# One PSUM bank for w and y of a linear recurrence, and a sum over gated branches by an accumulating DMA

## Chip, cores, metric

One core of a Trainium2 chip runs the kernel; the other cores are idle. The metric is the time of one execution on the device, in microseconds (us).

## What is computed

Two blocks of two layers each, in float32, on 256 tokens of width 1024. Each layer of the first block mixes three branches (sparse attention, a short convolution, and the linear recurrence of RWKV-7), then runs a gated feed-forward net. The change touches only this mixing. Cut to it:

```python
def step(state, inp):                       # the recurrence, per token and head (64 x 64 state)
    r_t, w_t, k_t, v_t, ka_t, kb_t = inp
    sa = jnp.einsum('bhvk,bhk->bhv', state, ka_t)
    state = (state * w_t[:, :, None, :] + sa[..., None] * kb_t[:, :, None, :]
             + v_t[..., None] * k_t[:, :, None, :])
    y_t = jnp.einsum('bhvk,bhk->bhv', state, r_t)
    return state, y_t
...
branches = jnp.stack([y_a, y_b, y_c], axis=2)
up = jnp.einsum('bsgc,gcd->bsgd', branches, w_branch[l])
gates = jax.nn.sigmoid(gate_pre + b_gate[l]).reshape(bsz, seq, N_BRANCH, D_MODEL)
mixed = jnp.sum(gates * up, axis=2)
h = h + mixed @ w_out[l]
```

## The kernel before

Weights stream from HBM in loads of up to 1 MB (`weights`, line 172, issued by SyncE). ScalarE (ACT) rounds each half to float32r (`whi`, line 184) and VectorE (DVE) takes the remainder (`wlo`, line 185); a product is then three float32r matmuls (lines 206 to 208 with the features on the partitions, 244 to 246 with the tokens on them). An operand is split in the same way (`split`, lines 198 and 199).

The first block's mixing (`mix`) runs three generators side by side: `rwkv`, `attend` and `bulk`. `bulk` makes the short convolution, then for 4 column pairs j the gate of branch 1 and its product, the gates of branch 2, then gate and product of branch 0, and last, after the recurrence is done, the product of branch 2. `branch` keeps the running sum: the first branch (g = 1) is written to m[j] (line 1035); each later one makes `u` = (tanh + 1) * up on DVE (line 1038) and GpSimd (POOL) adds it to m[j] (line 1039). After branch 2 each m[j] is halved on DVE (line 1083) and split into the operand `mg[j]` of the output projection (`residual`, whose matmuls are lines 244 to 246). The order of the instructions on one engine is set when the program is built, with due times and by dependences, and is not always that of the code; at run time each engine works in order.

The recurrence is done in 4 chunks of 64 tokens (`rw_chain`), 8 heads of 64. `ar` holds per chunk 64 columns for w and 64 for y (128 rows: two heads); `gm` holds masked scores with 128 rows (64 of the unknowns u, then 64 of the values v) and 128 columns (64 for w, 64 for y). In a chunk:

1. w = `ar`(first 64 columns) x old state + `gm`[64:128](first 64 columns) x v, lines 946 and 949, into one PSUM bank; chunk 0 has no state term. DVE copies it (`wsb`, line 951).
2. u = inverse x w, line 955; DVE copies it into rows 0 to 63 of `u2` (line 956); rows 64 to 127 hold v.
3. The new state, line 960, then DVE (lines 965, 966, 968).
4. y = `ar`(last 64 columns) x old state + `gm`(128 rows, last 64 columns) x `u2`, lines 973 and 976, into another bank; ACT copies it to `yc` (line 979).

After every second chunk `rw_finish` runs the group norm on `yc` (DVE with one ACT step; its reciprocal root is `rsqrt`, lines 261 to 271), and at the end `yc` is transposed (line 393) and split: that is the input of branch 2's product. The banks come from pool `rk`, which has two slots; a float32 matmul appears in the trace as two PE instructions.

Of the kernel before, what the change touches and what calls it, by code (L numbers as in the profile page):

```python
# [13 lines left out]
ALU = mybir.AluOpType  # L14
# [486 lines left out]
class Block1:  # L501
# [434 lines left out]
    def rw_chain(self):  # L936

        k, nc = self.k, self.k.nc
        ar, gm, bkt, uv, ti = self.ar, self.gm, self.bkt, self.uv, self.ti
        for c in range(4):  # L940
            s_old, s_new = self.sd[c % 2], self.sd[(c + 1) % 2]
            u2 = uv[c // 2][:, c % 2]
            ps = k.bank(k.rk, 8, 64)
            for hh in range(4):
                if c:
                    nc.tensor.matmul(ps[0:64, 2 * hh:2 * hh + 2], lhsT=ar[hh // 2][:, hh % 2, c, 0:64], rhs=s_old[:, hh], start=True, stop=False)
                for p in range(2):
                    h = 2 * hh + p
                    nc.tensor.matmul(ps[0:64, h], lhsT=gm[c][64:128, 4 * p + hh, 0:64], rhs=u2[64:128, 64 * h:64 * h + 64], start=c == 0, stop=c == 0 or p == 1)  # L949
            wsb = k.temp(8, 64, name="wsb")  # L950
            nc.vector.tensor_copy(wsb[0:64], ps[0:64])
            ps = k.bank(k.rk, 8, 64)
            for h in range(8):
                b = 8 * c + 4 * (h % 2) + h // 2
                nc.tensor.matmul(ps[0:64, h], lhsT=ti[:, b], rhs=wsb[0:64, h], start=True, stop=True)
            nc.vector.tensor_copy(u2[0:64], ps[0:64].rearrange("p a b -> p (a b)"))
            if c < 3:
                ps = k.bank(k.rk, 4, 128)
                for hh in range(4):
                    nc.tensor.matmul(ps[:, hh], lhsT=bkt[c // 2][:, c % 2, 128 * hh:128 * hh + 128], rhs=u2[:, 128 * hh:128 * hh + 128], start=True, stop=True)  # L960
                for p in range(2):
                    q = slice(64 * p, 64 * p + 64)
                    pc = self.pc[q, :, c:c + 1].to_broadcast([64, 4, 64])
                    if c:
                        nc.vector.tensor_tensor(out=s_new[q, :, q], in0=ps[q, :, q], in1=s_old[q, :, q], op=ALU.add)
                        nc.vector.tensor_tensor(out=s_new[q, :, q], in0=s_new[q, :, q], in1=pc, op=ALU.mult)
                    else:
                        nc.vector.tensor_tensor(out=s_new[q, :, q], in0=ps[q, :, q], in1=pc, op=ALU.mult)
            y = k.bank(k.rk, 8, 64)
            o = slice(64 * (c % 2), 64 * (c % 2) + 64)  # L970
            for hh in range(4):
                if c:
                    nc.tensor.matmul(y[o, 2 * hh:2 * hh + 2], lhsT=ar[hh // 2][:, hh % 2, c, 64:128], rhs=s_old[:, hh], start=True, stop=False)
                for p in range(2):
                    h = 2 * hh + p
                    nc.tensor.matmul(y[o, h], lhsT=gm[c][:, 4 * p + hh, 64:128], rhs=u2[:, 64 * h:64 * h + 64], start=c == 0, stop=c == 0 or p == 1)
            if c == 0:
                self.yc = k.slot(2, 512, name="yc")
            nc.scalar.copy(self.yc[o, c // 2].rearrange("p (h d) -> p h d", d=64), y[o])
            yield 8.0  # L980
            if c % 2:
                self.rw_finish(c // 2)
                yield 8.0
        yc = k.operand(2)
        for j in range(2):
            k.split(k.flip_pair([self.yc[:, 0], self.yc[:, 1]], j), *yc[j])
        self.yo = yc
        yield 3.0
# [41 lines left out]
    def branch(self, l, g, j, th, y, m):  # L1030

        k, nc = self.k, self.k.nc
        ps = k.feature_pair(self.w["w_branch"][l, g], 256 * j, y, 4)
        if m is None:
            nc.vector.scalar_tensor_tensor(out=th, in0=th, scalar=1.0, in1=ps, op0=ALU.add, op1=ALU.mult)
        else:
            u = k.temp(2, S, name="up")
            nc.vector.scalar_tensor_tensor(out=u, in0=th, scalar=1.0, in1=ps, op0=ALU.add, op1=ALU.mult)  # L1038
            nc.gpsimd.tensor_tensor(out=m, in0=m, in1=u, op=ALU.add)  # L1039
        return th  # L1040

    def rwkv(self, l):
# [439 lines left out]
```

## Time and profile before

| | us |
|---|---|
| median of 3 runs (1744.5 to 1745.21) | 1744.61 |
| profiled execution | 1742.93 |
| its span, first to last instruction | 1740.9 |
| busy PE / DVE / ACT / POOL | 1700.2 / 1250.7 / 957.2 / 72.4 |

Times in the profile count from the start of the span. A line of the timeline has start, duration, engine, source line, operation, output and inputs, shape, and in brackets how long the engine had been idle before it and what ended that. Consecutive instructions of one kind are merged into one line with their count (x16); the duration is then that of the whole run, and since matmuls are pipelined, their durations overlap. In the shape of a matmul, 64*128 means 64 contraction rows and 128 columns of the loaded operand.

### The profile page before, as it was taken

How to read it: one execution, taken by the hardware profiler on the slowest of the kernel's cores; microseconds unless marked ns; L12 is line 12 of the kernel's file. 1: busy time of each engine (PE TensorE's matmuls, PEld its weight loads, DVE VectorE, ACT ScalarE, POOL GpSimd, SP SyncE). 2: the span in 40 equal slices, each digit the busy share in tenths (PEclk: the TensorE clock that was granted, in tenths of full speed). 3: DMA queues.
4: the chain of work that ended last, by engine and by line, in shares of the span. 5: the costliest groups of instructions: out<-in, count | busy, mean ns of one | idle time of the engine just before them, and what ended most of it. 6: DMA issues, size and time to landing. Idle time of an engine off the chain costs nothing.

```text
span 1740.9 us, 30007 instructions
## 1 busy us (share of the span) xinstructions
PE 1700.2 (98%) x12016; PEld 1539.7 (88%) x12016; DVE 1250.7 (72%) x2464; ACT 957.2 (55%) x1688; POOL 72.4 (4%) x81
## 2 busy tenths in 40 slices
PE   8999899999999999899999999999999999999998
PEld 8988789899989988799899987788899887888997
DVE  6699947789957689757789857576666675666666
ACT  6554633556646544633555556666564566665643
POOL 2000201101000000201000000000000000000000
PEclk9999989999999999899999999999999999999999
DMA  7534323565556444314555565344445554444454
GB/s 229 171 111 128 115 74 101 178 192 186 181 179 209 127 137 129 98 62 146 169 189 177 186 211 170 129 157 142 157 147 172 191 172 144 146 149 158 155 171 134
DMA packets 217371, 268.89 MB, mean 154 GB/s; under 512 B 6570, under 2 KB 170716, under 8 KB 217232
## 3 DMA queue, kind: packets, MB, share of 16 engines
q1 hardware_dynamic: 213520, 262.81, 46.7%
q10 hardware_dynamic: 2944, 3.94, 0.8%
q8 instruction: 94, 1.54, 0.4%
q14 instruction: 45, 0.37, 0.1%
q0 software_dynamic: 768, 0.23, 0.1%
HBM read 265.91 MB, written 1.05 MB: 153 GB/s over the span
## 4 chain that ended last, share of the span: by engine, by line
PE 81%; DVE 11%; DMA 4%; ACT 3%; issue 2%; POOL 0%; ACTq 0%; SPq 0%; POOLq 0%; DVEq 0%
PE ps L206 15%; PE ps L207 15%; PE ps L208 15%; PE ps L246 8%; PE ps L244 8%; PE ps L245 8%; DVE wlo L185 4%; PE ps L445 2%; PE ps L393 2%; DMA raw<-in_ffn_down_dram 1%; DMA raw<-in_w_in_dram 1%; ACT whi L184 1%; PE ps L486 1%; DVE pr L905 1%; PE ps L949 1%
## 5 line engine op out<-in xcount | busy, mean ns | idle before, releaser
L185 DVE TENSOR_TENSOR wlo<-raw,whi 128x1024 fp32r<-128x1024 f32 (+2 forms) x504 | 615.4, 1224 | 302.2 <-ACT whi L184 289.1
L184 ACT ACTIVATE whi<-raw 128x1024 fp32r<-128x1024 f32 (+2 forms) x504 | 525.6, 1046 | 555.9 <-PE ps L207 292.8
L206 PE MATMUL ps<-op,whi 128*128 128x256 f32 x2464 | 710.6, 288 | 0.1
L207 PE MATMUL ps<-op,whi 128*128 128x256 f32 x2464 | 703.3, 285 | 1.2 <-DVE op L199 1.0
L208 PE MATMUL ps<-op,wlo 128*128 128x256 f32 x2464 | 702.2, 285 | 1.3 <-DVE wlo L185 1.2
L206 PEld LDWEIGHTS ps<-op,whi 128*128 128x128 f32 x2464 | 474.8, 193 | 11.2 <-issue 8.5
L207 PEld LDWEIGHTS ps<-op,whi 128*128 128x128 f32 x2464 | 475.2, 193 | 6.6 <-issue 4.3
L208 PEld LDWEIGHTS ps<-op,wlo 128*128 128x128 f32 x2464 | 474.9, 193 | 3.8 <-DVE wlo L185 1.8
L244 PE MATMUL ps<-whi,op 128*128 128x512 f32 (+2 forms) x784 | 306.2, 391 | 0.8 <-ACT qtok L1200 0.8
L245 PE MATMUL ps<-wlo,op 128*128 128x512 f32 (+2 forms) x784 | 302.2, 386 | 2.5 <-DVE wlo L185 2.5
L246 PE MATMUL ps<-whi,op 128*128 128x512 f32 (+2 forms) x784 | 303.2, 387 | 1.3 <-DVE op L199 1.3
L246 PEld LDWEIGHTS ps<-whi,op 128*128 128x128 f32 x784 | 148.5, 189 | 30.0 <-DVE op L199 2.2
L245 PEld LDWEIGHTS ps<-wlo,op 128*128 128x128 f32 x784 | 148.8, 190 | 29.4 <-DVE wlo L185 3.8
L244 PEld LDWEIGHTS ps<-whi,op 128*128 128x128 f32 x784 | 148.6, 190 | 29.4 <-issue 2.0
L454 ACT ACTIVATE e<-e,m 128x128 f32<-128x128 f32 (+1 forms) x160 | 70.9, 446 | 16.2 <-DVE m L451 15.8
L451 DVE CUSTOM_DVE_ANT_0 e<-ps,consts 128x128 f32<-128x128 f32 (+1 forms) x128 | 39.1, 351 | 15.5 <-PE ps L445 13.2
L199 DVE TENSOR_TENSOR op<-xt,op 128x512 fp32r<-128x512 f32 x48 | 32.2, 687 | 19.0 <-ACT op L198 18.8
L445 PE MATMUL ps<-qT 64*128 64x256 f32 (+1 forms) x256 | 35.8, 351 | 1.0 <-DVE m L451 0.8
L488 ACT COPY pt<-ps 128x384 f32<-128x384 f32 x64 | 28.8, 480 | 12.9 <-PE ps L486 7.6
L709 DVE SCALAR_TENSOR_TENSOR glu<-ps,vec,glu 128x254 f32<-128x254 f32 x72 | 34.4, 478 | 1.4
L1039 POOL TENSOR_TENSOR gate<-gate,up 128x512 f32<-128x512 f32 x16 | 26.0, 1627 | 212.3 <-DVE up L1038 169.6
L708 DVE SCALAR_TENSOR_TENSOR glu<-ps,vec,glu 128x255 f32<-128x255 f32 x72 | 34.3, 476 | 0.2
(337 smaller groups left out, 1562.7 us busy)
## 6 DMA issues: line engine op xcount, KB each, us to landing
raw<-in_w_in_dram SPq DMA_DIRECT2D x130, 1024.0 KB, 5.2
raw<-in_ffn_up_dram SPq DMA_DIRECT2D x44, 1024.0 KB, 5.1
raw<-in_ffn_down_dram SPq DMA_DIRECT2D x20, 1024.0 KB, 5.1
raw<-in_w_out_dram SPq DMA_DIRECT2D x16, 1024.0 KB, 5.2
raw<-in_w_branch_dram SPq DMA_DIRECT2D x24, 512.0 KB, 3.4
raw<-in_w_proj_a_dram SPq DMA_DIRECT2D x8, 1024.0 KB, 5.2
raw<-in_w_proj_b_dram SPq DMA_DIRECT2D x8, 1024.0 KB, 5.2
raw<-in_w_in_dram SPq DMA_DIRECT2D x8, 768.0 KB, 4.4
```

Of the source, the lines that this page charges most:

```text
L184: nc.scalar.activation(out=hi, in_=v, func=AF.Copy)
L185: nc.vector.tensor_tensor(out=lo, in0=v, in1=hi.bitcast(F32), op=ALU.subtract)
L206: self.nc.tensor.matmul(ps, lhsT=hi[:, k], rhs=xh, start=k == 0, stop=False)
L207: self.nc.tensor.matmul(ps, lhsT=hi[:, k], rhs=xl, start=False, stop=False)
L208: self.nc.tensor.matmul(ps, lhsT=lo[:, k], rhs=xh, start=False, stop=k == nk - 1)
L244: self.nc.tensor.matmul(ps[t][:, :n], lhsT=xh, rhs=hi, start=kk == first, stop=False)
L245: self.nc.tensor.matmul(ps[t][:, :n], lhsT=xh, rhs=lo, start=False, stop=False)
L246: self.nc.tensor.matmul(ps[t][:, :n], lhsT=xl, rhs=hi, start=False, stop=kk == last)
L393: self.nc.tensor.transpose(ps[:, a, 128 * t:128 * t + 128], src[t][:, 128 * k:128 * k + 128], self.ident)
L445: nc.tensor.matmul(ps[b][:, a:a + n], lhsT=qt[r, 128 * t:128 * t + 128], rhs=kt[r, 0:n], start=True, stop=True)
L451: nc.vector.tensor_tensor_reduce(out=e[:, a:a + n], in0=ps[b][:, a:a + n], in1=mask[:, a:a + n], scale=1.0, scalar=3e38, op0=ALU.add, op1= ...
L454: nc.scalar.activation(out=e[:, a:a + n], in_=e[:, a:a + n], func=AF.Exp, scale=-1.0, bias=m[:, t:t + 1], accum_out=z[:, 2 * b + t:2 * b + ...
```

## The change

In `rw_chain` w and y share one bank `wy`: w's matmuls load all 128 columns of `gm` and `ar`, so that rows 0 to 63 of the bank get w and rows 64 to 127 the part of y that needs only v and the old state. All `gm` matmuls stand together ahead of all `ar` matmuls. When u is known, y gets only the remaining term, with 64 contraction rows. The separate bank and the 4 `ar` matmuls of y in chunks 1 to 3 are gone. In `branch` the POOL add becomes a DMA, issued by POOL, that reads `u` and adds it to m[j] in SBUF.

```diff
-            ps = k.bank(k.rk, 8, 64)
-            for hh in range(4):
-                if c:
-                    nc.tensor.matmul(ps[0:64, 2 * hh:2 * hh + 2], lhsT=ar[hh // 2][:, hh % 2, c, 0:64], rhs=s_old[:, hh], start=True, stop=False)
-                for p in range(2):
-                    h = 2 * hh + p
-                    nc.tensor.matmul(ps[0:64, h], lhsT=gm[c][64:128, 4 * p + hh, 0:64], rhs=u2[64:128, 64 * h:64 * h + 64], start=c == 0, stop=c == 0 or p == 1)
+
+            wy = k.bank(k.rk, 8, 64)
+            for h in range(8):
+                nc.tensor.matmul(wy[:, h], lhsT=gm[c][64:128, 4 * (h % 2) + h // 2], rhs=u2[64:128, 64 * h:64 * h + 64],
+                                 start=h == 0, stop=False, skip_group_check=True)
+            if c:
+                for hh in range(4):
+                    nc.tensor.matmul(wy[:, 2 * hh:2 * hh + 2], lhsT=ar[hh // 2][:, hh % 2, c], rhs=s_old[:, hh],
+                                     start=False, stop=False, skip_group_check=True)
             wsb = k.temp(8, 64, name="wsb")
-            nc.vector.tensor_copy(wsb[0:64], ps[0:64])
+            nc.vector.tensor_copy(wsb[0:64], wy[0:64])
...
-            y = k.bank(k.rk, 8, 64)
             o = slice(64 * (c % 2), 64 * (c % 2) + 64)
-            for hh in range(4):
-                if c:
-                    nc.tensor.matmul(y[o, 2 * hh:2 * hh + 2], lhsT=ar[hh // 2][:, hh % 2, c, 64:128], rhs=s_old[:, hh], start=True, stop=False)
-                for p in range(2):
-                    h = 2 * hh + p
-                    nc.tensor.matmul(y[o, h], lhsT=gm[c][:, 4 * p + hh, 64:128], rhs=u2[:, 64 * h:64 * h + 64], start=c == 0, stop=c == 0 or p == 1)
+            for h in range(8):
+                nc.tensor.matmul(wy[64:128, h], lhsT=gm[c][0:64, 4 * (h % 2) + h // 2, 64:128], rhs=u2[0:64, 64 * h:64 * h + 64],
+                                 start=False, stop=h == 7, skip_group_check=True)
             if c == 0:
                 self.yc = k.slot(2, 512, name="yc")
-            nc.scalar.copy(self.yc[o, c // 2].rearrange("p (h d) -> p h d", d=64), y[o])
+            nc.scalar.copy(self.yc[o, c // 2].rearrange("p (h d) -> p h d", d=64), wy[64:128])
...
             u = k.temp(2, S, name="up")
             nc.vector.scalar_tensor_tensor(out=u, in0=th, scalar=1.0, in1=ps, op0=ALU.add, op1=ALU.mult)
-            nc.gpsimd.tensor_tensor(out=m, in0=m, in1=u, op=ALU.add)
+            nc.gpsimd.dma_start(out=m, in_=u, accum_op=ALU.add)
```

## Rows read from the trace of the kernel before

**Rows 1.** The page: shares of the chain that ended last; the costliest group

```profile
PE 81%; DVE 11%; DMA 4%; ACT 3%; issue 2%; POOL 0%; ACTq 0%; SPq 0%; POOLq 0%; DVEq 0%
...
L185 DVE TENSOR_TENSOR wlo<-raw,whi 128x1024 fp32r<-128x1024 f32 (+2 forms) x504 | 615.4, 1224 | 302.2 <-ACT whi L184 289.1
```

**Rows 2.** Waits of PE: us in total, times, longest

```profile
PE ps L393 <- DVE yc L1020: 2.9, 2, 1.4
...
PE ps L246 <- DVE op L199: 1.3, 2, 0.7
```

**Rows 3.** Timeline of PE, recurrence, chunk 2 of the first layer

```profile
253.82 0.43 PE L946 MATMUL ps<-sd,ar 128*64 128x128 f32 x2
...
254.56 0.43 PE L946 MATMUL ps<-sd,ar 128*64 128x128 f32 x2
...
258.02 1.14 PE L955 MATMUL ps<-wsb,ti 64*64 64x64 f32 x16
260.15 1.06 PE L960 MATMUL ps<-uv,bkt 128*128 128x128 f32 x8
...
261.64 0.38 PE L973 MATMUL ps<-sd,ar 128*64 128x128 f32 x2
...
262.09 0.38 PE L973 MATMUL ps<-sd,ar 128*64 128x128 f32 x2
```

**Rows 4.** Timeline of PE: other small float32 matmuls, and chunk 0

```profile
217.78 0.80 PE L926 MATMUL ps<-t,gm 32*32 32x32 f32 x11
...
610.53 1.18 PE L808 MATMUL ps<-consts,kn 128*128 128x8 f32 x10
...
655.59 1.16 PE L861 MATMUL ps<-ar,bk 64*128 64x128 f32 x16
...
737.76 1.97 PE L949 MATMUL ps<-uv,gm 64*64 64x64 f32 x16
...
745.21 1.91 PE L960 MATMUL ps<-uv,bkt 128*128 128x128 f32 x8
747.06 1.63 PE L976 MATMUL ps<-uv,gm 128*64 128x64 f32 x16
```

**Rows 5.** Windows (us; busy PE, PEld, DVE, ACT, POOL; PEclk; DMA share; GB/s)

```profile
218.00:220.00 2.00, 2.00 (x27) 1.68 (x25) 0.00 (x0) 1.37 (x4) 0.00 (x0) 0.77 0.83 262
...
232.00:234.00 2.00, 2.00 (x24) 1.76 (x23) 0.67 (x2) 0.59 (x2) 0.00 (x0) 0.81 0.00 0
```

**Rows 6.** Timeline of DVE and POOL in the group norm, first layer

```profile
288.83 0.17 DVE L275 TENSOR_SCALAR gn<-gn 128x8 f32<-128x8 f32 x1
...
288.99 1.28 POOL L1039 TENSOR_TENSOR gate<-gate,up 128x512 f32<-128x512 f32 x1 [7.24 <-DVE gn L275]
289.03 1.28 DVE L261 TENSOR_SCALAR rsy<-gn 128x8 int32<-128x8 int32 x1
```

**Rows 7.** Timeline of DVE at the end of the first mixing stage

```profile
300.28 2.17 DVE L185 TENSOR_TENSOR wlo<-raw,whi 128x1024 fp32r<-128x1024 f32 x1 [0.28 <-ACT whi L184]
302.37 0.67 DVE L1038 SCALAR_TENSOR_TENSOR up<-gate,ps 128x512 f32<-128x512 f32 x1
303.16 2.33 DVE L185 TENSOR_TENSOR wlo<-raw,whi 128x1024 fp32r<-128x1024 f32 x1
305.41 0.41 DVE L1083 TENSOR_SCALAR gate<-gate 128x512 f32<-128x512 f32 x1
...
315.60 1.77 DVE L199 TENSOR_TENSOR op<-gate,op 128x512 fp32r<-128x512 f32 x1
```

**Rows 8.** Windows of the same stage

```profile
298.00:311.00 13.00, 13.00 (x109) 12.96 (x108) 10.87 (x13) 5.67 (x8) 4.38 (x3) 1.00 0.58 204
311.00:323.00 12.00, 11.27 (x50) 8.79 (x48) 10.22 (x13) 5.04 (x6) 4.28 (x2) 1.00 0.49 165
```

**Rows 9.** DMA issues: queue, count, KB each, median us to landing

```profile
gup<-in_rw_g_up_dram ACTq DMA_DIRECT2D x2, 256.0 KB, 4.4
...
out_dram<-hg SPq DMA_DIRECT2D x2, 256.0 KB, 2.1
```

## Prediction

> **What bounds the kernel now.** I read the page first. The matrix engine (PE) carries 81% of the chain that ended last, VectorE (DVE) 11% [rows 1]. So an instruction taken from PE gives back its pitch (start to start), not its listed duration, since durations overlap; and a step on another engine counts only where PE stands waiting for it. The change has two places, each once per layer of the first block, so I read those next: the recurrence by the timeline of PE, and the end of the mixing stage by the waits, the timelines of DVE, POOL and PE, and the windows. Around the recurrence other work fills PE's waits, so there the price is PE pitch alone. At the end of mixing PE waits twice in each of the two layers: up to 1.4 us for `yc`, the end of the recurrence, and up to 0.7 us for an operand made from the sum over branches [rows 2].
>
> **w and y in one bank.** Every float32 matmul is two PE instructions. In chunks 1 to 3 the old w is four groups of two `L946` and four `L949`, and a group comes every 0.74 us (253.82 to 254.56), 2.94 us in all. The old y is four groups of two `L973` and four `L976`, 0.45 us each (261.64 to 262.09), 1.80 us in all [rows 3]. The groups of w are longer because PE goes from 128 contraction rows to 64 and back in each of them: 0.74 less 0.45 is some 0.28 us for the two switches.
>
> New w: 16 instructions with 64 rows and 128 columns, then 8 with 128 by 128. No row has the first shape with 64 moving columns. Its pitch is bounded below by 0.06 us, which `L861` shows with two alternating row halves ((1.16 - 0.27) / 15), and above by 0.11 us from `L960` ((1.06 - 0.28) / 7); the nearest is `L808`, 128 columns loaded for 8 moving ones, (1.18 - 0.28) / 9 = 0.10 us [rows 3, 4]. I take 0.10. That is 1.60 + 0.28 + 8 x 0.11 = 2.76 us against 2.94 (bounds 2.1 and 2.9). New y: 16 instructions of 64 by 64 at the pitch of `L955`, (1.14 - 0.22) / 15 = 0.061, plus a switch pair: 0.98 + 0.28 = 1.26 us against 1.80. One chunk gains 0.18 + 0.54 = 0.72 us, and six chunks 4.3 us (bounds 3.5 and 8.3).
>
> Chunk 0 goes the other way. It has no `L946`, so nothing is merged, and its w loads 128 columns where it loaded 64. It also runs on the low clock: the granted clock falls to 1.2 GHz in the stretch from 218 us and is back at 2.4 GHz in that from 232 us [rows 5]; before the fall PE ran matmuls of 32 by 32 [rows 4]. Old w there is 16 at 0.118 = 1.9 us; new w lies between the same 1.9 and 16 x 0.23 = 3.7 us, the pitch of `L960` at that clock ((1.91 - 0.3) / 7) [rows 4]. I take 3.2, nearer the row with as many columns: +1.3 us. Old y there took some 1.4 us (1.63 less one overlap) [rows 4]; new y is 16 x 0.118 = 1.9 us, less if the clock rises within it: +0.5 us (bounds -0.2 and +0.7). Chunk 0 loses 1.8 us (-0.2 to +2.5), two layers 3.6 us. The first part comes to 3.6 - 4.3 = **-0.7 us**, bounds -8.7 and +1.5.
>
> One PSUM slot of the two of `rk` is now held from w to the copy of y. The state update takes the other, which its own input (`u2`) has freed already, so I price that at nothing; were it to wait, the wait would be a VectorE copy, some 0.7 us a chunk.
>
> **The sum by DMA.** Sixteen POOL adds (`L1039`) go and sixteen accumulating DMAs of 256 KB, issued by POOL, come. POOL's other work of the layer (`rw_rows`, the memsets) stands ahead of them and the next layer's far behind, so none of it is delayed. Two effects, per layer:
>
> *What goes.* While POOL adds, DVE work is slow. An eight-column operation of `rsqrt` (`L261`) took 1.28 us beside an add that began 0.04 us earlier; its neighbour took 0.17 us [rows 6]. It lies on the group norm's path to `yc`, for which PE then waits 1.4 us [rows 2]. So 1.1 us of that wait goes: **-2.2 us** for two layers (0 to -2.5; 0 if issuing the DMA blocks DVE as the add does, or if the order of DVE's work changes there).
>
> *What comes.* The four sums of branch 2 are each followed by the halving (`L1083`), the split (ACT, then DVE) and the output projection. Now 2.37 us pass from the end of the product (302.37 + 0.67) to the halving at 305.41 [rows 7]. With a DMA they must hold its issue, its reading of both operands and its landing. No row shows an accumulating DMA. From below: storing 256 KB lands in 2.1 us. From above: a 256 KB load beside other traffic lands in 4.4 us [rows 9], and the second operand is another 256 KB; at full share the traffic here is some 204 / 0.58 = 350 GB/s [rows 8], so 0.75 us alone and 1.5 us shared with the weight loads, hence 6 us. I take 4.5, near the loaded row, since the stage also streams `w_out`.
>
> The halving waits in DVE's queue, and behind it stand the next product, the low halves (`wlo`) of the `w_out` weights and the next split, for which PE waits. From 298 to 323 us DVE is busy for 10.87 + 10.22 = 21.1 of 25 us, so it has 3.9 us idle [rows 8]; without the POOL adds it gets some 3.1 us more: `wlo` at 303.16 takes 2.33 us and at 300.28 2.17, where the mean of its line is 1.22, and the split at 315.60 takes 1.77 us, some 1.1 more than its kind does alone [rows 1, 7]. Four halvings, each 4.5 - 2.37 = 2.1 us later, need 8.5 us; 7.0 are there. So 1.5 us per layer reach PE: **+3.0 us**. At 2.1 us nothing waits, and PE's 0.7 us for the operand goes too: -1.5 us. At 6 us it is 4 x 3.63 - 7.0 = 7.5 us per layer, +15 us. The eight sums of branch 0 have many us until they are read; they cost nothing, and if they did, it would show as a wait of the first halving.
>
> The Trainium skill, DMA: Bandwidth & Descriptors, section "Anatomy of one DMA — SWDGE (gpsimd) path", fits a DMA issued by GpSimd as 2.0 us plus bytes over 436 GB/s. That would be an estimate of 2.6 us here, and by it the last term would be -1.5 instead of +3.0. The trace's loaded rows are slower, and I go by them.
>
> **The sum.** -0.7 - 2.2 + 3.0 = +0.1 us. The profiled execution took 1742.93 us (span 1740.9 and 2.0 around it); the median of the three timed runs lies 1.7 us above it, and I put the sum on the median: **1744.7 us, no change**. This kernel's measurement can tell some 0.2%, 3.5 us, from no change.
>
> **Rivals.** *The DMA is slow (slower).* Place: the four halvings at the end of mixing. It decides from a latency of some 5 us; at 5.3 us the four waits exceed the cover by 4 x 2.93 - 7.0 = 4.7 us a layer, 9.4 us in all, less the 2.9 gained elsewhere 6.5 us: 1751. At 6 us it is 1757. For it: four 1 MB loads of `w_out` are under way in the same 20 us. Against it: the halving already stands behind other DVE work, and the order could put more there. The skill's page SBUF — State Buffer, section "Who interferes with whom", says that descriptors of GpSimd's DMAs are held up by DVE's two-port modes; no row here shows it. Chance 0.26.
>
> *The clock comes back late (slower).* The low stretch ends just after PE ran full-array matmuls (`L960`) and y [rows 4, 5]. The new y has half the rows. If y and the next w stayed at 1.2 GHz, they would cost some 3.5 us per layer more: 1752. Against it: chunk 0's w now fills twice the columns, which could as well bring the clock back sooner. Chance 0.08.
>
> *The DMA is quick (faster).* Near the store's 2.1 us nothing waits: -0.7 - 2.2 - 1.5 = -4.4, 1740; with the low bound of w's pitch as well, 1732. For it: no HBM is read. Chance 0.22. This is also what the skill's fit above would give.
>
> *The change doesn't do what it says:* if other work splits up the merged matmuls in PE's order, the switches stay; the first part then gives up to +3 us, still within the forecast. Chance 0.04, and 0.40 for the forecast itself.
>
> **How the numbers follow.** Faster by over 0.2%: 0.22. Within 0.2%: 0.40 + 0.04 = 0.44. Slower: 0.26 + 0.08 = 0.34. The range takes in most of both sides, 1738 to 1755; it leaves out the double gain below and the slowest DMAs above. The likeliest case's own range is 1741 to 1748.
>
> **What would show it.** In the changed profile: `L949` with 128 columns at a pitch of 0.10 us and y at 0.06; `L261` back at 0.17 us and PE's wait for `yc` near 0.3 us; DVE's wait before `L1083` naming a DMA; that DMA's landing time, 4.5 us, in the list of DMA issues. The prediction is wrong if that landing is under 3 or over 5.3 us, if the granted clock returns at another point of chunk 0 or 1, or if DVE's order changes so that the halving no longer holds anything up.

## The result: slower by 0.7%, and the profile after

The changed kernel takes 1755.76 us (median of four runs, 1752.95 to 1760.66) against 1744.55 us (1742.09 to 1745.21): 11.2 us more, a ratio of 1.0069 with a 95% interval of 1.0052 to 1.0085. The forecast of 1744.7 us was wrong, and its range ended at 1755, 0.8 us short. The profiled execution took 1756.67 us, with a span of 1754.9.

Where the time went is seen first by stage. For each layer of the first block I take two points of PE's timeline: the first `L926`, just ahead of the recurrence, and the first transpose of the new `h` (`L393`), which ends the mixing.

| us | start to `L926` | recurrence to end of mixing, layer 1 | to `L926` of layer 2 | the same stage, layer 2 | rest |
|---|---|---|---|---|---|
| before | 214.8 | 108.3 | 405.8 | 109.4 | 902.6 |
| after | 213.7 | 116.5 | 404.0 | 119.7 | 901.1 |

All of the loss lies in the two stages that the change touches, 8.2 and 10.3 us; elsewhere the profiled execution was a little quicker.

First the page: the shares of the chain, and the row of the new DMA among the issues (count, KB, median us to landing). It lands in 4.2 us, close to the 4.5 that the prediction took, and this median misleads, as will be seen.

```profile
PE 82%; DVE 9%; issue 4%; DMA 3%; ACT 2%; POOL 0%; SPq 0%; POOLq 0%; ACTq 0%; DVEq 0%
...
gate<-up POOLq DMA_DIRECT2D x16, 256.0 KB, 4.2
```

The waits (us in total, times, longest) answer to [rows 2]:

```profile
ACT op L198 <- DVE gate L1081: 22.1, 8, 7.2
DVE gate L1081 <- DMA gate<-up: 17.8, 8, 4.5
PE ps L244 <- ACT op L198: 5.4, 3, 3.0
PE ps L245 <- DVE wlo L185: 4.6, 7, 1.2
PE ps L946 <- ACT yc L977: 1.4, 2, 0.7
PE ps L246 <- DVE op L199: 1.0, 3, 0.3
PE ps L393 <- DVE yc L1018: 0.8, 2, 0.4
```

Two lines of the kernel before, to be held against the second and the fourth:

```profile
DVE gate L1083 <- POOL gate L1039: 4.7, 4, 1.2
PE ps L245 <- DVE wlo L185: 2.5, 4, 1.2
```

Read from the last line up: the wait for `yc` fell from 1.4 to 0.4 us a layer. A new wait of 0.7 us a layer stands before w of chunk 1 (`L946`), and the halving (`L1081`) waits in every one of its eight places for the DMA, behind it ACT for the operand, behind that PE. Behind the operand (`L198`) stand the high halves of the weights (`whi`) in ACT's queue, so in the first layer PE's first long wait names them. The first load of `w_out`, issued at 302.84 us, had landed by then, after 7.0 us.

```profile
311.62 0.63 ACT L198 ACTIVATE op<-gate 128x512 fp32r<-128x512 f32 x1 [7.19 <-DVE gate L1081]
312.16 1.99 ACT L184 ACTIVATE whi<-raw 128x1024 fp32r<-128x1024 f32 x2
313.25 0.50 PE L244 MATMUL ps<-whi,op 128*128 128x512 f32 x1 [1.16 <-ACT whi L184]
```

The timeline of DVE at the end of the first mixing stage, to be held against [rows 7]:

```profile
303.49 0.69 DVE L1036 SCALAR_TENSOR_TENSOR up<-gate,ps 128x512 f32<-128x512 f32 x1 [0.68 <-PE ps L208]
304.46 1.23 DVE L185 TENSOR_TENSOR wlo<-raw,whi 128x1024 fp32r<-128x1024 f32 x1 [0.29 <-ACT whi L184]
306.37 0.69 DVE L1036 SCALAR_TENSOR_TENSOR up<-gate,ps 128x512 f32<-128x512 f32 x1 [0.68 <-PE ps L208]
311.16 0.43 DVE L1081 TENSOR_SCALAR gate<-gate 128x512 f32<-128x512 f32 x1 [4.10 <-DMA gate<-up]
...
314.95 0.43 DVE L1081 TENSOR_SCALAR gate<-gate 128x512 f32<-128x512 f32 x1 [0.49 <-DMA gate<-up]
...
320.59 0.43 DVE L1081 TENSOR_SCALAR gate<-gate 128x512 f32<-128x512 f32 x1 [1.15 <-DMA gate<-up]
...
325.08 0.43 DVE L1081 TENSOR_SCALAR gate<-gate 128x512 f32<-128x512 f32 x1 [2.33 <-DMA gate<-up]
```

Two things are new. The second product (306.37) now stands ahead of the first halving; before, the halving came right behind the low halves. And `wlo` takes 1.23 us where it took 2.17 and 2.33. Next POOL, which issues the sums; the row of SP's loads of `w_out` in the same time; and the windows of two stretches (us; busy PE, PEld, DVE, ACT, POOL; PEclk; DMA share; GB/s):

```profile
301.60 0.85 POOL L1037 DMA_DIRECT2D gate<-up  x1 [9.15 <-DVE up L1036]
304.47 0.85 POOL L1037 DMA_DIRECT2D gate<-up  x1 [2.02 <-DVE up L1036]
307.36 0.85 POOL L1037 DMA_DIRECT2D gate<-up  x1 [2.03 <-DVE up L1036]
316.26 0.85 POOL L1037 DMA_DIRECT2D gate<-up  x1 [8.05 <-DVE up L1036]
318.60 0.86 POOL L1037 DMA_DIRECT2D gate<-up  x1 [1.48 <-DVE up L1036]
...
302.84 19.70 SPq L172 DMA_DIRECT2D raw<-in_w_out_dram  x4
...
306.00:311.00 5.00, 5.00 (x44) 5.00 (x44) 0.69 (x1) 0.00 (x0) 0.85 (x1) 1.00 1.07 288
320.00:325.00 5.00, 3.35 (x11) 2.01 (x10) 2.16 (x3) 1.69 (x2) 0.00 (x0) 0.85 1.05 316
```

The trace gives a landing time for each issue. Earlier in the layer (issues at 269.1, 283.0 and 291.6) they are 4.2, 3.7 and 3.6 us. The five above land after 4.4, 6.7, 7.6, 4.3 and 6.5 us, and the last of the second layer after 8.5: a sum issued 2.3 to 2.9 us behind another takes longer (5.4 to 8.5 us) than one with none ahead (3.6 to 4.4), and the DMA engines are full where the halving waits longest, with DVE busy for 0.69 of 5 us. The loads of `w_out` suffer too: the four of this stage land after 7.0, 10.0, 6.7 and 7.4 us, where the same four took 5.1 to 5.2 in the kernel before. The median of 4.2 is that of a mixed population: half of it are sums of branch 0, most of them in quiet stretches.

Last, the recurrence: PE in chunk 0 and the start of chunk 1 (to 240 us), then chunk 2 of the first layer, and the windows.

```profile
222.14 3.67 PE L946 MATMUL ps<-uv,gm 64*128 64x64 f32 x16
...
232.61 1.97 PE L973 MATMUL ps<-uv,gm 64*64 64x64 f32 x16
235.29 3.67 PE L946 MATMUL ps<-uv,gm 64*128 64x64 f32 x16 [0.72 <-ACT yc L977]
238.89 2.07 PE L950 MATMUL ps<-sd,ar 128*128 128x128 f32 x8
...
258.26 2.00 PE L946 MATMUL ps<-uv,gm 64*128 64x64 f32 x16
260.19 1.16 PE L950 MATMUL ps<-sd,ar 128*128 128x128 f32 x8
...
266.19 1.14 PE L973 MATMUL ps<-uv,gm 64*64 64x64 f32 x16
...
218.00:234.00 16.00, 16.00 (x134) 14.94 (x133) 3.44 (x5) 4.00 (x8) 0.00 (x0) 0.50 0.05 17
234.00:242.00 8.00, 7.28 (x37) 6.88 (x35) 1.37 (x2) 3.37 (x8) 0.00 (x0) 0.53 0.00 0
```

Before, the clock of the first layer was back at 2.4 GHz in the window from 232 us [rows 5]; now it comes back near 241, so w of chunk 1 also runs at 1.2 GHz: 235.29 to 240.62 (the next instruction), 5.3 us, where chunk 2 takes 2.84 (258.26 to 261.10). The second layer goes another way: y of chunk 0 runs at full clock, PE waits 0.72 us, and the clock falls again within w of chunk 1, which takes 4.2 us (755.66 to 759.82).

```profile
753.80 1.14 PE L973 MATMUL ps<-uv,gm 64*64 64x64 f32 x16
755.66 2.50 PE L946 MATMUL ps<-uv,gm 64*128 64x64 f32 x16 [0.72 <-ACT yc L977]
758.09 2.07 PE L950 MATMUL ps<-sd,ar 128*128 128x128 f32 x8
```

Summed over windows of 2 us, PE ran at the low clock for the equivalent of 23.9 us in the first layer and 23.8 in the second (13.7 and 17.1 before).

### The profile page after: what moved, and what is told of

It reads as the page before. It is cut to its first block, busy times and chain, and to the rows that moved or that the text cites. A ratio compares the mean times of both kernels' runs of the same rounds, so it can differ in the third digit from the quotient of the medians.

```text
span 1754.9 us, 29929 instructions
## 1 busy us (share of the span) xinstructions
PE 1706.5 (97%) x11968; PEld 1546.4 (88%) x11968; DVE 1239.6 (71%) x2464; ACT 958.3 (55%) x1688; POOL 61.1 (3%) x81
## 4 chain that ended last, share of the span: by engine, by line
PE 82%; DVE 9%; issue 4%; DMA 3%; ACT 2%; POOL 0%; SPq 0%; POOLq 0%; ACTq 0%; DVEq 0%
PE ps L206 15%; PE ps L207 15%; PE ps L208 14%; PE ps L246 9%; PE ps L244 9%; PE ps L245 9%; DVE wlo L185 2%; PE ps L445 2%; PE ps L393 2%; DMA raw<-in_w_in_dram 1%; PE ps L946 1%; PE ps L486 1%; DVE pr L905 1%; PE ps L496 1%; DMA gate<-up 1%
## 5 line engine op out<-in xcount | busy, mean ns | idle before, releaser
L185 DVE TENSOR_TENSOR wlo<-raw,whi 128x1024 fp32r<-128x1024 f32 (+2 forms) x504 | 608.5, 1210 | 306.5 <-ACT whi L184 289.2
L246 PEld LDWEIGHTS ps<-whi,op 128*128 128x128 f32 x784 | 148.3, 189 | 30.8 <-DVE op L199 2.6
L486 PE MATMUL ps<-ident,e 128*128 128x128 f32 x192 | 31.7, 287 | 3.5 <-DVE m L451 3.5
```

The costliest lines, as they stand in the source:

```text
L185: nc.vector.tensor_tensor(out=lo, in0=v, in1=hi.bitcast(F32), op=ALU.subtract)
L246: self.nc.tensor.matmul(ps[t][:, :n], lhsT=xl, rhs=hi, start=False, stop=kk == last)
L486: self.nc.tensor.transpose(ps[:, 128 * j:128 * j + 128], p[:, 128 * j:128 * j + 128], self.ident)
```

## The experiments

Each was timed beside the kernel before on its own chip; differences are medians against that chip's median of before (1742.86 us for the four kernels of the next two sections; 1743.27 for the DMA by branch and for the bank with DVE's sums or with DMA and POOL; 1744.89 for the halves, the folded halving, DVE's sums on the old chain and the bank with DMA and DVE; 1744.12 for every second sum and for the last version). "Low time" is the low-clock equivalent just described, for both layers, in the one profiled execution of a kernel; before has 30.8 us, and the kernels with the old chain below have 30.6 to 41 us, so a difference of some us says little by itself.

### The two parts apart

**One bank alone**: the changed kernel with POOL's add put back.

```diff
-            nc.gpsimd.dma_start(out=m, in_=u, accum_op=ALU.add)
+            nc.gpsimd.tensor_tensor(out=m, in0=m, in1=u, op=ALU.add)
```

> The bank of w and y alone; the sum stays on POOL. Theory A (both parts cost): the low clock around chunk 0 lasts as long as in the changed kernel (returns near 241.5 us instead of 232.8 in the first layer, and some 5 us later in the second). Some 14 us more at half speed lose 7 us of PE work, against 4.3 us gained in chunks 1 to 3: 2 to 4 us slower than before. Theory B (only the DMA costs): within 1 us of before, and the long low stretch is seen only together with the DMA. Theory C (only the recurrence costs): 9 to 12 us slower, the whole of the change.

Measured: 1746.95 us, +4.1, ratio 1.0021 (1.0012 to 1.0029); low time 47.7 us. The stage grew by 2.7 and 2.2 us. The low clock isn't one long stretch here, as expected, but two: the clock is back near 233 us in the first layer, PE waits 0.72 us ahead of w of chunk 1 (235.15), and near 236 the clock falls again (PEclk, third number from the end):

```profile
232.00:234.00 2.00, 2.00 (x20) 1.88 (x20) 0.57 (x2) 0.00 (x0) 0.00 (x0) 0.77 0.00 0
234.00:236.00 2.00, 1.28 (x16) 1.15 (x13) 0.27 (x1) 1.47 (x4) 0.00 (x0) 1.00 0.00 0
236.00:238.00 2.00, 2.00 (x12) 1.88 (x11) 0.69 (x1) 1.90 (x5) 0.00 (x0) 0.58 0.00 0
```

**The DMA alone**: the kernel before with this line changed.

```diff
-            nc.gpsimd.tensor_tensor(out=m, in0=m, in1=u, op=ALU.add)
+            nc.gpsimd.dma_start(out=m, in_=u, accum_op=ALU.add)
```

> The sum by DMA alone; the recurrence as before. Theory A: DVE waits for the DMA before each halving of branch 2, 4 to 8 us a layer, and PE after it; against it the wait for yc shrinks by 1 us a layer: 6 to 9 us slower than before. Theory B: 9 to 12 us slower. Theory C: within 2 us of before. The clock near 219 to 233 us should be that of before in all of them.

Measured: 1752.04 us, +9.2, ratio 1.0049 (1.0037 to 1.0061). The stage grew by 5.9 and 5.0 us, DVE waited 16.9 us for the sums in seven places. Both parts lose, and 4.1 + 9.2 = 13.3 is, within the intervals, the 11.2 of both.

### The bank: chunk 0

**Chunk 0 in its old shapes**, chunks 1 to 3 in one bank as changed, POOL's add:

```diff
+                if c:
                     nc.tensor.matmul(wy[:, h], lhsT=gm[c][64:128, 4 * (h % 2) + h // 2], rhs=u2[64:128, 64 * h:64 * h + 64],
                                      start=h == 0, stop=False, skip_group_check=True)
+                else:
+                    nc.tensor.matmul(wy[0:64, h], lhsT=gm[c][64:128, 4 * (h % 2) + h // 2, 0:64], rhs=u2[64:128, 64 * h:64 * h + 64],
+                                     start=h == 0, stop=h == 7, skip_group_check=True)
...
+                if c:
                     nc.tensor.matmul(wy[64:128, h], lhsT=gm[c][0:64, 4 * (h % 2) + h // 2, 64:128], rhs=u2[0:64, 64 * h:64 * h + 64],
                                      start=False, stop=h == 7, skip_group_check=True)
+                else:
+                    nc.tensor.matmul(wy[64:128, h], lhsT=gm[c][:, 4 * (h % 2) + h // 2, 64:128], rhs=u2[:, 64 * h:64 * h + 64],
+                                     start=h == 0, stop=h == 7, skip_group_check=True)
```

> One bank for w and y in all chunks, but chunk 0 has its matmuls in the shapes of before (w with 64 columns, y with 128 rows); chunks 1 to 3 as changed; the sum on POOL. Theory D (the shape of chunk 0 holds the clock low): the clock returns at 2.4 GHz near 233 us as before, and the 4.3 us of chunks 1 to 3 are seen: 2 to 4.5 us faster than before. Theory E (sharing the bank, by PE's wait for the copy of y, holds it low): the clock returns near 241 us as in the changed kernel, and the time is 1 to 4 us slower than before.

Measured: 1741.82 us, -1.0, ratio 0.9991 (0.998 to 1.0002), low time 34.1 us, in the fastest of its twelve executions (1737.30). In layer 1 of that one the clock now returns where it did before and stays; in layer 2 it falls once more, for the equivalent of 3.4 us. Against the bank as changed the time is 5.1 us less: taking back chunk 0's shapes takes back the whole loss of this part. The gain over before is smaller than expected and not told apart from nothing. What keeps it small, by an estimate: the wait for the slot stays, 1.4 us in two layers, and the granted clock, averaged over all executions, is 0.9836 against 0.9852 for before on the same chip, which is 0.0016 of 1743 us, 2.8 us of work. Together that is 4.2 of the 5.0 us that six chunks gain at full clock (0.83 us each, below).

**Only y of chunk 0 in its old shape**, w of chunk 0 with 128 columns:

```diff
+                if c:
                     nc.tensor.matmul(wy[64:128, h], lhsT=gm[c][0:64, 4 * (h % 2) + h // 2, 64:128], rhs=u2[0:64, 64 * h:64 * h + 64],
                                      start=False, stop=h == 7, skip_group_check=True)
+                else:
+                    nc.tensor.matmul(wy[64:128, h], lhsT=gm[c][:, 4 * (h % 2) + h // 2, 64:128], rhs=u2[:, 64 * h:64 * h + 64],
+                                     start=h == 0, stop=h == 7, skip_group_check=True)
```

> As the kernel with the bank alone, but y of chunk 0 with 128 contraction rows and 64 columns, as before; w of chunk 0 with 128 columns, as changed (its upper half of the bank is not used then). Theory D1 (the half-height y keeps the clock down): the clock returns some 2 us after the point of before, 235 us, and the time is 1 to 3 us faster than before. Theory D2 (the wide w keeps it down, by being slower and later): the clock returns near 241 us, 1 to 4 us slower than before.

Measured: 1744.09 us, +1.2, ratio 1.0004 (0.9995 to 1.0012), low time 40.9 us: midway. The wide w is worth 2.3 of the 5.1 us (1744.09 less 1741.82), the half-height y 2.9, each uncertain by some 2 us (an estimate from the spread of the executions). Rows of PE, layer 1, in the kernel with chunk 0 in its old shapes (first two) and the one with only y old (last two):

```profile
222.56 1.97 PE L950 MATMUL ps<-uv,gm 64*64 64x64 f32 x16
232.96 2.00 PE L947 MATMUL ps<-uv,gm 64*128 64x64 f32 x16 [0.71 <-ACT yc L985]
```

```profile
222.55 3.67 PE L946 MATMUL ps<-uv,gm 64*128 64x64 f32 x16
235.56 2.00 PE L946 MATMUL ps<-uv,gm 64*128 64x64 f32 x16 [0.72 <-ACT yc L981]
```

In both, the `gm` part of w of chunk 1 runs at full clock again (2.00 us, not 3.67), and the wide w of chunk 0 costs 1.7 us at the low clock. The wait of 0.7 us for the copy of y stays in both. The granted clock, averaged over all executions, is the same in these two kernels, 0.9836 and 0.9835, and 0.9812 with the bank as changed. So the half-height y goes together with a lower clock; the wide w, by these averages, does not, and costs what it takes at the low clock. Why the clock is higher with y in its old shape was not tried further.

Theory E of the expectation above (PE's wait for the copy of y holds the clock low) is not settled by this. The changed kernel and the seven others here with one bank have 16 places (two layers each) in which PE waits 0.7 us for the slot ahead of w of chunk 1. In 14 of them the clock, back at 2.4 GHz by then, falls again some 1 to 2.5 us after that w began, for the equivalent of 3.4 or 6.8 us. The other two are layer 1 of the changed kernel, where it was not back yet, and layer 1 of the kernel with chunk 0 in its old shapes, where it stayed up. The eight kernels with two banks, before among them, show no second fall behind chunk 0. So it goes with the shared bank, with chunk 0 in its old shapes too. Whether the wait brings it about or the new shapes behind it is not shown. Chunk 2 has the same shapes without the wait and ran at full clock (258.26, above), which speaks for the wait, but no kernel had the bank with a third slot.

### The DMA: which sums cost

**DMA for branch 0 only**, and **for branch 2 only** (old chain, POOL's add for the other). The diff is the first's; the second has the two calls the other way round.

```diff
+            if g == 0:
+                nc.gpsimd.dma_start(out=m, in_=u, accum_op=ALU.add)
+            else:
                 nc.gpsimd.tensor_tensor(out=m, in0=m, in1=u, op=ALU.add)
```

> The kernel before, with the DMA only for the eight sums of branch 0; branch 2 keeps its POOL add. Theory A (the DMA costs only where a halving waits for it at once, at the end of mixing): within 2 us of the kernel before, because the sums of branch 0 are read many us later; if its adds were what slowed the group norm, PE's wait for yc falls from 1.4 to some 0.4 us, and the time by 1 to 2 us. Rival B (256 KB through the DMA engines delays the loads of weights wherever it runs): 3 us or more slower.

> The kernel before, with the DMA only for the eight sums of branch 2. Theory A: as slow as with all sixteen, 7 to 11 us slower than before, with DVE waiting some 17 us for the sums and landings of 5 to 8 us. Rival B: about half of that, 3 to 6 us.

Measured: branch 0 alone 1740.26 us, -3.0, ratio 0.9979 (0.997 to 0.9988); branch 2 alone 1752.69, +9.4, ratio 1.0046 (1.0028 to 1.0064), as much as all sixteen. So a DMA whose result is read many us later costs nothing and, by taking POOL off the group norm, gains: PE's wait for `yc` fell from 2.9 to 1.6 us in two layers. That is 1.3 of the 3.0 us; the rest is not traced, though the `wlo` beside the last sum of branch 0 took 1.23 us instead of the 2.17 of [rows 7]. And a DMA whose result is awaited carries the whole loss. In the kernel with branch 2, the first sum of each layer, with no other sum ahead of it, landed after 6.4 and 7.6 us, beside the loads of `w_out`; the second, 3.0 us behind it, after 7.7 and 7.8.

**Half the bytes**: two DMAs of 128 KB in branch 0, one of 128 KB in branch 2, where the kernel leaves out the other half of each sum.

```diff
-            nc.gpsimd.tensor_tensor(out=m, in0=m, in1=u, op=ALU.add)
+            nc.gpsimd.dma_start(out=m[:, 0], in_=u[:, 0], accum_op=ALU.add)
+            if g == 0:
+                nc.gpsimd.dma_start(out=m[:, 1], in_=u[:, 1], accum_op=ALU.add)
```

> The kernel before, with DMAs of half the size: in branch 0 two of 128 KB, one issued behind the other; in branch 2 one of 128 KB, and the sum of the second 128 rows of each pair in branch 2 is left out. It measures the landing that the prediction took as 4.5 us. Theory A (at the end of mixing the sum shares the DMA engines with four loads of 1 MB, so its bytes decide): the landings in branch 2 fall from 4.5 to 7.8 us to 3 to 5, VectorE's wait for them from 17 to 8 us or less, and the time is 2 to 5 us above before instead of 8. Rival B (a fixed time for each DMA that its size does not change): landings over 4.5 us stay, the wait stays over 13 us and the time 7 to 9 us above before.

Measured: 1750.17 us, +5.3, ratio 1.0036 (1.0022 to 1.005); DVE's wait for the sums 11.1 us. The four landings of branch 2 in layer 1 were 5.9, 6.0, 3.0 and 4.6 us against 6.4, 7.7, 4.5 and 6.0 with 256 KB. (The first of them stood behind the last pair of branch 0, so its 0.5 us is a lower bound.) That is between the two theories: half the bytes take 0.5 to 1.7 us off, so bytes count, but most of the landing stays. The pairs of branch 0 tell something more: the first of a pair landed after 2.7 to 3.9 us in layer 1, the second, issued some 0.5 us later, after 5.3 to 6.9. Two halves, one behind the other, take longer than one whole (3.6 to 4.4). The second seems to be served after the first, not beside it; that is tried below.

**Folding the halving into the split** (DMA for branch 2, POOL's add for branch 0):

```diff
-            k.nc.vector.tensor_scalar(out=m[j], in0=m[j], scalar1=0.5, scalar2=None, op0=ALU.mult)
-            k.split(m[j], *mg[j])
+            k.nc.scalar.activation(out=mg[j][0], in_=m[j], func=AF.Copy, scale=0.5)
+            k.nc.vector.scalar_tensor_tensor(out=mg[j][1], in0=m[j], scalar=0.5, in1=mg[j][0].bitcast(F32), op0=ALU.mult, op1=ALU.subtract)
```

> The kernel before with the DMA for branch 2 alone, and the halving folded into the split (ScalarE copies half of the sum, VectorE takes half of the sum less that copy), so that no instruction of VectorE waits for the DMA directly. Theory Q (the cost is that the halving waits at the head of VectorE's queue and holds up the low halves and the next product): within 3 us of before. Rival L (the cost is the landing itself, since TensorE needs each split operand and the next one comes no earlier): 5 to 9 us slower, TensorE's wait for the operand of the split unchanged at some 5 us.

Measured: 1748.63 us, +3.7, ratio 1.0026 (1.0014 to 1.0038); the stage grew by 3.8 and 4.5 us, with the halving by 6.2 and 6.3. Again between the theories, so both carry part. The waits of this kernel show where the rest went: the sums are as late as ever, and now ACT stands waiting for them, and DVE for ACT.

```profile
ACT op L1086 <- DMA gate<-up: 27.4, 8, 7.3
...
DVE op L1087 <- ACT op L1086: 18.0, 6, 5.3
```

So 3.7 of the 9.4 us of the DMA for branch 2 stay when DVE no longer waits for it (each against before on its own chip); by the stages it is 8.3 of 12.4 us, in single executions. Which part is the larger is not settled. The other is what the edit took from DVE's queue, the wait and eight instructions of 0.43 us; this run does not split these two.

**Every second sum of branch 2 by DMA**, all others by DVE:

```diff
-            nc.gpsimd.tensor_tensor(out=m, in0=m, in1=u, op=ALU.add)
+            if g == 2 and j % 2:
+                nc.gpsimd.dma_start(out=m, in_=u, accum_op=ALU.add)
+            else:
+                nc.vector.tensor_tensor(out=m, in0=m, in1=u, op=ALU.add)
```

> The kernel before with the old chain; of the four sums of branch 2 in a layer, the second and the fourth by DMA, all other sums by VectorE. To be compared with VectorE's sums alone, 1737.3 us. Theory F (DMAs of one queue are served one behind the other, at some 4 us each, so a sum issued 2.3 to 3.0 us after another waits for it): with no sum ahead of them the second lands in 4 to 5.5 us instead of 7.7 and the fourth in 3.5 to 4.7 instead of 6.0, and the time is 1739 to 1744. Rival C (the loads of w_out beside it alone make it slow): landings of 6 to 8 us stay, 1744 or more.

Measured: 1742.73 us, -1.4, ratio 0.9996 (0.9987 to 1.0006), where DVE's sums alone have -7.6 (below): 6.2 us lost, each against before on its own chip. The line of its four DMAs:

```profile
DMA to landing us min/median/max: 3.9/4.7/5.9
```

The fourth sums land after 4.0 and 3.9 us instead of 6.0 (layer 1, branch 2 by DMA); the second after 5.3 and 5.9 instead of 7.7 and 7.8. So having no sum ahead takes off some 2 us, as theory F has it. The second sum of layer 2, at 5.9, misses its 5.5, and both second sums stay 1.3 to 2 us above the fourth. That the share of the DMA engines explains this can't be said: it was 0.86 around the second sum (305 to 311 us) and 0.98 around the fourth (315 to 319). What makes a lone sum land after 4 us in one place of the stage and after 5.3 to 7.6 in another stays open. Even so, two sums a layer with a landing near 4.7 us cost some 6 us in all.

The Trainium skill, DMA: Bandwidth & Descriptors, section "Queues, rings and completion order", has each DMA engine take turns, packet by packet, between the queues that have work. The trace agrees in direction, since sums and loads both land later where they meet (sums 5.3 to 7.6 us with none ahead, against 3.6; loads 6.7 to 10.0, against 5.1), but not in size everywhere, as the fourth sums show. The fit that the prediction quoted from that page, an estimate of 2.6 us, was reached by no sum of 256 KB: the quickest landed after 3.6 us.

### Who else could add

**DVE's sums on the old chain**:

```diff
-            nc.gpsimd.tensor_tensor(out=m, in0=m, in1=u, op=ALU.add)
+            nc.vector.tensor_tensor(out=m, in0=m, in1=u, op=ALU.add)
```

> The kernel before with its old chain of w and y, only the sum moved from POOL to VectorE. If the gain of the version with one bank and VectorE's sums is the end of the contention between POOL and VectorE, most of it is here: 5 to 8 us faster. If it is the bank with the old chunk 0, this stays within 2 us of before.

Measured: 1737.33 us, -7.6, ratio 0.9964 (0.9951 to 0.9976). So POOL's add, which looks free because POOL has nothing else to do, cost more than sixteen more instructions on the second busiest engine. Rows: DVE in this kernel, the add and the low halves behind it (against 2.17 and 2.33 us in [rows 7]), then POOL's add in the kernel with the DMA for branch 0 only:

```profile
302.36 0.69 DVE L1039 TENSOR_TENSOR gate<-gate,up 128x512 f32<-128x512 f32 x1
302.97 1.22 DVE L185 TENSOR_TENSOR wlo<-raw,whi 128x1024 fp32r<-128x1024 f32 x1
```

```profile
309.06 2.21 POOL L1042 TENSOR_TENSOR gate<-gate,up 128x512 f32<-128x512 f32 x1 [3.35 <-DVE up L1038]
```

The add takes 0.69 us on DVE and from 1.28 to 2.21 on POOL. At the end of mixing, which of the two engines is slowed goes by which began first. The add at 303.12 us in the kernel before, just ahead of the `wlo` of 2.33 us in [rows 7], took 1.29; a later one, 0.22 us behind a `wlo`, was the slow one:

```profile
311.13 1.22 DVE L185 TENSOR_TENSOR wlo<-raw,whi 128x1024 fp32r<-128x1024 f32 x1
311.35 2.14 POOL L1039 TENSOR_TENSOR gate<-gate,up 128x512 f32<-128x512 f32 x1 [2.98 <-DVE up L1038]
```

The Trainium skill, SBUF — State Buffer, section "Who interferes with whom", says that an instruction of DVE with two inputs in SBUF contends with one of GpSimd that reads SBUF; `wlo` is such a one, and its 2.17 and 1.22 us agree.

**The bank with chunk 0 in its old shapes, with other sums**: DVE's for all; the DMA for branch 0 and POOL for branch 2; the DMA for branch 0 and DVE for branch 2; and DVE's for all with the halving folded as above.

> w and y in one bank with chunk 0 in its old shapes, and the sum made by VectorE behind the product. No POOL add stands beside VectorE, and nothing crosses to another engine ahead of a halving. If the contention of two engines at SBUF is what the POOL add costs, the twelve slow operations of VectorE return to their shorter times (the copy of the low halves 2.2 to 1.2 us) and pay for the add of some 1.1 us: 1 to 4 us faster than the kernel before. If VectorE is too full at the end of mixing, where it had 3.9 us idle in 25, the four adds push the splits back and it is 0 to 4 us slower.

> w and y in one bank with chunk 0 in its old shapes, the DMA for branch 0 alone, POOL's add for branch 2. Theory A: what the bank gave by itself in this form (1 us) and what leaving POOL out of the group norm gives (1 to 2 us): 1 to 4 us faster than before. Rival B (the DMA costs wherever it runs): 2 us slower or more.

> w and y in one bank with chunk 0 in its old shapes, the DMA for branch 0, VectorE's add for branch 2: POOL adds nowhere. Theory A (what POOL's adds cost is their contention with VectorE, and VectorE has room for the adds): as fast as with VectorE's add in both branches, 6 to 9 us faster than before, or 1 us better where VectorE is spared eight adds. Rival B: VectorE's adds cost time in the recurrence too, and with eight of them gone it is 10 us faster or more.

> w and y in one bank with chunk 0 in its old shapes, VectorE's sums, and the halving folded into the split. Eight instructions of 0.43 us go from VectorE's queue at the end of mixing: 0 to 3 us faster than the same version with the halving (8 us faster than before), so 8 to 11 us faster than before, if VectorE's queue sets when the last operands are there; 8 if not.

| | us | ratio (95%) |
|---|---|---|
| DVE for all | 1735.63 | 0.9953 (0.9937 to 0.9969) |
| DMA, POOL | 1738.60 | 0.9971 (0.9959 to 0.9982) |
| DMA, DVE | 1735.35 | 0.9949 (0.9935 to 0.9962) |
| DVE for all, folded | 1734.41 | 0.9943 (0.9928 to 0.9958) |

All beat both kernels; the last is the fastest, 9.7 us under before and 21 under the change. The first two gained more than expected, 7.6 and 4.7 us against 1 to 4. But the bank adds nothing that can be told to DVE's sums: 7.6 us with it, 7.6 without. The DMA for branch 0 neither helps nor harms once DVE can add. The order among the three fastest, 1 us apart, is not settled.

## Why the prediction was wrong, by its own steps

**What bounds the kernel** held: the loss came where PE stood waiting, or ran slowly, in the two places named, and nowhere else.

**w and y in one bank: -0.7 us predicted, +4.1 measured.** The pitches were right. New w takes 2.84 us at full clock against 2.76 predicted (pitch (2.00 - 0.28) / 15 = 0.115, not 0.10), new y 1.07 us (266.19 to 267.26) against 1.26; the gain of a full-speed chunk is 0.10 + 0.73 = 0.83 us where 0.72 was predicted. Chunk 0 itself lost what was said, 1.7 us for w (predicted 1.3) and, in the first layer, some 0.5 for y. The step that failed is the clock, and a wait with it. In the first layer the clock came back some 9 us later, and w of chunk 1 lost 2.5 us by it (5.3 less 2.84); in the second it came back within chunk 0 and fell again, and w of chunk 1 lost 1.3 (4.2 less 2.84). That is the rival priced at 3.5 us a layer and given a chance of 0.08, though a second fall was no part of it. I weighed the wide w as likely to bring the clock back sooner; no run shows that. What the runs show is a lower clock with the half-height y, and the second fall in nearly every place where the bank is shared; what brings it about stays open. And the shared slot, priced at nothing, cost 0.72 us a layer: w of chunk 1 needs the slot that y of chunk 0 holds until ACT has copied it, since the state update has the other. The prediction named VectorE's copy as the one to fear; it was ACT's, and only once a layer.

**What goes: -2.2 us predicted, -2.1 measured** at the place named, in PE's wait. `L261` is back at 0.17 us, in this row of the changed kernel, to be held against [rows 6]:

```profile
291.42 0.17 DVE L261 TENSOR_SCALAR rsy<-gn 128x8 int32<-128x8 int32 x1
```

PE's wait for `yc` fell by 2.1 us (with the bank alone it stayed at 3.0), and the kernel with the DMA in branch 0 alone gained 3.0 us in time.

**What comes: +3.0 us predicted, some +11 measured** (9.2 for the DMA alone, and the 2.1 that the contention gave back). The step that failed is the size of one term, the latency. I took 4.5 us from rows of single loads, with an upper bound of 6. In the eight places that count the landings were 6.7, 7.6, 4.3, 6.5 and 5.4, 7.3, 4.1, 8.5 us, 6.3 on average: above the bound, since the row of a single load holds no sum ahead of it on the same queue (some 2 us, by the experiment with every second sum) and none of this stage's traffic. The working gives the sign, not the size: put in 25.1 and 25.3 us for the four sums of a layer, and 25.1 - 4 x 2.37 - 7.0 = 8.6 and 8.8, 17.4 in all. That is too much by 6. It counts each wait in full, though a sum was under way while the one ahead was awaited (304.47 to 311.17 us and 307.36 to 314.96); that this makes up all of the 6 us is not shown. The slow rival gave 1751 at 5.3 us and 1757 at 6; for the DMA alone that is +7.2 and +12.8 (9.4 and 15 less 2.2), and the measured +9.2 lies between. That the whole change came out near the rival's upper end is luck, since the bank's part lay 4.8 us above its forecast. The rival's reason, the loads of `w_out` in the same 20 us, is one of two; the queue of sums was in no step.

**DVE's order.** The prediction held it open and called it a way to be wrong. The second product now stands ahead of the first halving; that helps the second sum (0.49 us of wait) and leaves the first wait at 4.10. The Trainium skill's sentence in the prediction on descriptors held up by DVE (SBUF — State Buffer, section "Who interferes with whom") has no support here: POOL's issue took 0.85 to 0.93 us in all sixteen.

**What would show it.** Of the three signs that the prediction named as proof against it, one is there as named, the clock back at another point. The landing is over 5.3 us in the eight places that count, but not in the list of DMA issues, where the prediction looked for it (4.2). DVE's order changed, but the halving still holds up what stands behind it.

**The chances.** The two slower cases had 0.34 together, as if one excluded the other. Nothing in them excludes the other; both came true, and the time lies outside a range that held either alone up to 1755, but not the two together.

## What to carry to other kernels

A DMA as an adder was free here only where nobody read the sum soon: price it at the place where it is awaited, with the other transfers of that stretch and the sums issued just ahead of it, not by a single transfer or by the median over all its places. An add on an idle engine isn't free either when it and a busy engine hold each other up: here sixteen adds cost less on the busy engine. And merging small matmuls took 0.83 us off a chunk at full clock, but no run shows a gain in time from it. Where nothing was merged, twice the columns took nearly twice the time (3.67 against 1.97 us for sixteen instructions at 1.2 GHz), and sharing a bank between an early and a late use made the next chunk wait for the slot.

## What the hardware showed that I had not expected

- An accumulating DMA of 256 KB within SBUF landed after 3.6 to 4.2 us ahead of the end of mixing in the changed kernel (up to 5.1 in the kernel with the DMA alone), 3.9 to 7.6 at the end of mixing with no other ahead, and up to 8.5 behind another; its issue holds POOL for 0.85 to 0.93 us.
- PE's clock stayed at 1.2 GHz, or fell to it again, in stretches in which PE was given matmuls almost without pause: 7.28 of 8 us busy from 234 to 242, at a granted clock of 0.53.
- Of a POOL add and a DVE instruction with two operands in SBUF, the one that began first ran at its own pace (1.29 us, 1.22 us) and the other was slowed (to 2.33 us, to 2.14).
- At the end of mixing the clock fell as well in the changed kernel, behind PE's waits of 1.31 and 0.34 us (to 321.73 and 322.80). In the kernel with the DMA alone, which has such waits too (1.08 and 0.34 us), it did not. In the changed kernel:

```profile
322.00:328.00 6.00, 5.66 (x17) 3.95 (x17) 2.91 (x5) 2.72 (x3) 0.00 (x0) 0.72 0.83 249
```
